# Forming the weight sums of the seven products by accumulating DMAs

## The chip, the cores and the metric

The kernel runs on one core of one Trainium2 chip. The metric is the device time of one execution in microseconds (us). TensorE (PE in the profile) multiplies, PEld is its weight load, VectorE is DVE, ScalarE is ACT, GpSimd is POOL, and SyncE (SP) issues most DMAs. An engine works through its own instructions in order; semaphores tie the engines and the DMAs together.

## The reference

One inference step of a one-layer streaming encoder with 1024 prompt tokens and 64 sample tokens (T = 1088 columns in all), D_MODEL = 1024, D_FF = 2816, everything in float32:

```python
def merge_branches(ret_o, ret_g, swa_o, gate_a, gate_b, w_ret_out, w_swa_out, w_mix_out):
    a = (rms_norm(ret_o) * silu(ret_g)) @ w_ret_out
    b = swa_o @ w_swa_out
    return (sigmoid(gate_a) * a + sigmoid(gate_b) * b) @ w_mix_out

rq, rk, rv, rg, sq, sk, sv, ga, gb = split(rms_norm(x, g_attn) @ w_in)
x = x + merge_branches(retention(rope(rq), rope(rk), rv), rg, window_attention(sq, sk, sv), ga, gb, ...)
x = x + cross_attn(rms_norm(x, g_cross), memory)
hn = rms_norm(x, g_ffn)
x = x + (silu(hn @ w_gate) * (hn @ w_up)) @ w_down
y = rms_norm(x, g_final)
```

The change touches the products with w_in, w_gate, w_up and w_down.

## The kernel before

Activations lie transposed: features on the 128 partitions, the 1088 tokens along the row. A float32 factor is split into two parts of the type float32r, hi and lo (`split`, L122): ScalarE casts hi (L123), VectorE subtracts it from the source to get lo (L124). A product is then three matmuls, hi·hi, hi·lo and lo·hi (L212, L213, L215).

The large products go in pairs of output tiles. A pair is a 2 x 2 block product: A is the weights' two output tiles (rows i) by two halves of the inner dimension (columns j), each block 128 partitions x 512 columns, 256 KB; B is the activations, two inner halves by two token halves of 544 columns. Instead of eight block products the kernel makes seven (Strassen's scheme in Winograd's form). One such group of seven is called a set here. There are 59 of them: 28 in the projection phase (q, k and v of the retention, queries and keys and values of the window attention, three gates), 21 for gate and up, 10 for the down projection. A set's seven products are named P1, P2, P6, P5, P7, P3, P4 in the order in which TensorE makes them. P1, P2 and P4 take the blocks A11, A12, A22 as they are; the others take sums of blocks. The sums of the activations (B11, B21, T2, T1, T3, B22, T4) are formed once for many sets.

For each set two raw tiles come from memory by SP (`load_raws`, L867; the down projection has its own loads): the first holds A11 and A12, the second A21 and A22. The pool has two such tiles (tag "raw", bufs=2), so one set's raws at a time. `weight_ops` (L173) splits the blocks that are used as they are, and POOL forms the sums in place: L190 A11 = A11 − A21, L191 A21 = A21 + A22, L193 A11 = A22 − A11, L196 A12 = A12 − A11. Each operand gets a tile "wq" (`new_op`, L144): five of them, and a sixth from the gates on; a tile is free when the product that read it is done, so splits run at most that many products ahead of TensorE. P7's operand is formed before P6's and P5's, though its product comes after them; `new_op` counts for this in its argument `ahead`.

`strassen` (L254) makes the products. Their results are joined on VectorE as they come out of PSUM: u1 is a copy of P1 (L262, ScalarE, once a set), u2 = P6 + u1, u5 = P5 + u2, u3 = P7 + u2 (L259), and each of the four output blocks is one more addition, in the callback `emit`, which each phase has of its own: in the projections `taken` (L591, its addition is L596), in gate and up `gate` and `up` (L1459, L1467), in the down projection `add` (L1542).

POOL also scales projections by the token's root mean square (L602), multiplies the gates a second time by it (L1465), forms the four sums of the hidden activations that go to memory for the down projection (L1480 to L1489) and adds to the outputs of the down projection (L1547). It issues a few DMAs, among them four stores of a gate (L697). The last group of the down projection has inner halves of three blocks (384 columns) and skips P2 and P4, so a set there has five products.

The order on each engine is made when the program is built: a scheduler that replays a timeline of its own places the instructions by their priority and expected time.

Of the kernel before, what the change touches and what calls it, by code (L numbers as in the profile page):

```python
# [109 lines left out]
class Kernel:  # L110
# [61 lines left out]

    def weight_ops(self, raws, n=512, skip=()):  # L173

        nc = self.nc
        half = [[raws[i][:, j * n:(j + 1) * n] for j in range(2)] for i in range(2)]
        (a11, a12), (a21, a22) = half
        add, sub = ALU.add, ALU.subtract
        w = {}

        def put(name, src):
# [3 lines left out]
            self.split(src, q[:, 0, :n], q[:, 1, :n])  # L185

        tt = nc.gpsimd.tensor_tensor
        put("P1", a11)
        put("P2", a12)
        tt(out=a11, in0=a11, in1=a21, op=sub)  # L190
        tt(out=a21, in0=a21, in1=a22, op=add)  # L191
        put("P7", a11)
        tt(out=a11, in0=a22, in1=a11, op=sub)  # L193
        put("P6", a11)
        put("P5", a21)
        tt(out=a12, in0=a12, in1=a11, op=sub)  # L196
        put("P3", a12)
        put("P4", a22)
        return w
# [54 lines left out]
    def strassen(self, w, x, emit, part=False):  # L254


        nc = self.nc
        u1, u2, u3, u5 = (self.fp.tile([P, 2, HC], F32, tag=t, bufs=1, name=t) for t in ("u1", "u2", "u3", "u5"))
        add = lambda out, a, b: nc.vector.tensor_tensor(out=out, in0=a, in1=b, op=ALU.add)  # L259
        ps = self.product(w, x, "P1", "B11")  # L260
        self.run_later()
        nc.scalar.copy(u1, ps)  # L262
# [307 lines left out]
    def project_phase(self):  # L570
        nc, tc, io = self.nc, self.tc, self.io
        with ExitStack() as ctx:
# [17 lines left out]

            def taken(ps, sb):  # L591
                o = staged()
                if sb is None:
                    nc.scalar.copy(o, ps)
                else:
                    nc.vector.tensor_tensor(out=o, in0=ps, in1=sb, op=ALU.add)  # L596
                return flat(o)

            def project(w, put, act=None, other=None):
                def emit(i, t, ps, sb):  # L600
                    o = taken(ps, sb)
                    (nc.vector if act is not None else nc.gpsimd).tensor_tensor(  # L602
# [12 lines left out]
            def rotated(w, h, j):  # L615

                done = {}

                def emit(i, t, ps, sb):
                    done[i, t] = taken(ps, sb)  # L620
                    if (1 - i, t) not in done:
# [16 lines left out]
            def values(w, h, by=self.strassen):  # L638
                def emit(i, t, ps, sb):
                    self.store(self.d_qkv[2, 2 * h + i, :, half(t)], taken(ps, sb))  # L640
                by(w, self.ops, emit)
# [233 lines left out]
    def load_ops(self, srcs):  # L875
        return self.weight_ops(self.load_raws(srcs))

# [555 lines left out]
    def gate_up(self, pairs):  # L1433
# [16 lines left out]
        for n, fs in enumerate(pairs):  # L1450
# [7 lines left out]

            def gate(i, t, ps, sb):  # L1459
                g = gates[i, t]  # L1460
                if sb is not None:
                    nc.vector.tensor_tensor(out=g, in0=ps, in1=sb, op=ALU.add)
# [4 lines left out]
            def up(i, t, ps, sb, h=h, save=save, n=n):  # L1467
                o = stage[4 + 2 * i + t]
                nc.vector.tensor_tensor(out=o, in0=ps, in1=sb, op=ALU.add)
                nc.vector.tensor_tensor(out=o, in0=o, in1=gates[i, t], op=ALU.mult)  # L1470
# [64 lines left out]
    def down(self, starts):  # L1535
# [28 lines left out]
        for gi, g in enumerate(GROUPS):  # L1564
            last = gi == len(GROUPS) - 1
            f0, n = starts[gi], g * P // 2
            for m in range(0, KT, 2):
                def emit(i, t, ps, sb, m=m):
                    add(m, i, t, ps, sb, nc.vector if last else nc.gpsimd)
                    if last and t == 1:  # L1570
# [15 lines left out]
                else:  # L1586
                    w = self.weight_ops(raws, n, ("P2", "P4") if last else ())
                    if m == KT - 2 and not last:
# [200 lines left out]
```

## Time and profile before

| | before |
|---|---|
| runs (us) | 2219.13, 2220.92, 2227.09 |
| median (us) | 2220.92 |
| span of the profiled execution (us) | 2221.3 |
| bytes moved by DMA | 290.84 MB, mean 131 GB/s |

The profiled execution's time is known as its span; it lies 0.4 us over the median of the three runs. The page lists each engine's busy time, the span in 40 slices, the DMA queues, the chain of work that ended last and the costliest groups of instructions. By slices (busy tenths, 55.5 us each):

```profile
PE   9999899999999998999999999999999999999996
DVE  8996778777677668765455555768777777778498
POOL 1221534342144122220000000014556555424440
DMA  5533445343444566326443112422343332385233
```

The sets lie in slices 1 to 15 (projections and gates) and 27 to 39 (gate and up, then down). A line of a group reads: line, engine, operation, out<-in, count | busy us, mean ns of one | idle time of the engine before them, and what ended it.

### The profile page before, as it was taken

What the parts mean: (1) busy time and instruction counts of PE and PEld (TensorE: products, weight loads), DVE (VectorE), ACT (ScalarE), POOL (GpSimd) and SP (SyncE); (2) the same over time, 40 slices, a digit from 0 to 9 for tenths busy, and PEclk for the clock granted to TensorE, in tenths of its full rate; (3) what the DMA queues carried; (4) which work ended last, traced back from release to release, by engine and by line L of the source; (5) the groups of instructions that cost most, each with busy time, mean ns of one, the idle gap of its engine ahead of it and who ended that gap; (6) DMA issues with size and microseconds to landing.
All of it is one profiled execution on the core that took longest, in us unless ns stands there. A gap on an engine that the chain in (4) does not pass through costs nothing. (4 is left out here: it accounts for less than half of the span.)

```text
span 2221.3 us, 41708 instructions
## 1 busy us (share of the span) xinstructions
PE 2165.5 (97%) x16435; PEld 2102.8 (95%) x16435; DVE 1573.4 (71%) x2654; ACT 887.8 (40%) x1900; POOL 643.1 (29%) x442
## 2 busy tenths in 40 slices
PE   9999899999999998999999999999999999999996
PEld 9999899999999996779999999999999999999996
DVE  8996778777677668765455555768777777778498
ACT  7334343435444446554133333333323222334243
POOL 1221534342144122220000000014556555424440
PEclk9999999999999999999999999999999999999998
DMA  5533445343444566326443112422343332385233
GB/s 202 161 112 113 119 130 143 108 135 112 151 158 164 171 216 216 99 69 210 137 151 101 69 40 66 140 89 89 120 134 102 103 119 94 129 289 170 87 113 110
DMA packets 181445, 290.84 MB, mean 131 GB/s; under 512 B 40290, under 2 KB 109314, under 8 KB 181250
## 3 DMA queue, kind: packets, MB, share of 16 engines
q1 hardware_dynamic: 176706, 278.74, 39.7%
q10 hardware_dynamic: 4032, 7.80, 0.9%
q8 instruction: 130, 2.13, 0.4%
q0 software_dynamic: 512, 1.64, 0.2%
q14 instruction: 65, 0.53, 0.1%
HBM read 196.95 MB, written 91.16 MB: 130 GB/s over the span
## 5 line engine op out<-in xcount | busy, mean ns | idle before, releaser
L123 ACT CAST wq<-raw 128x512 fp32r<-128x512 f32 (+1 forms) x499 | 303.6, 613 | 583.2 <-PE pq L215 251.0
L124 DVE TENSOR_TENSOR wq<-raw,wq 128x512 fp32r<-128x512 f32 (+1 forms) x499 | 436.7, 878 | 137.8 <-ACT wq L123 136.2
L212 PE MATMUL pq<-T,wq 128*128 128x272 f32 x1832 | 494.0, 289 | 3.9 <-ACT wq L123 1.9
L213 PE MATMUL pq<-T,wq 128*128 128x272 f32 x1832 | 494.1, 289 | 0.0
L213 PE MATMUL pq<-B,wq 128*128 128x272 f32 x1592 | 430.9, 290 | 6.9 <-DVE B L124 6.9
L212 PE MATMUL pq<-B,wq 128*128 128x272 f32 x1592 | 428.4, 289 | 1.9 <-DVE stage L596 1.9
L215 PE MATMUL pq<-T,wq 128*128 128x272 f32 x1832 | 384.7, 290 | 0.0
L190 POOL TENSOR_TENSOR raw<-raw 128x512 f32<-128x512 f32 (+1 forms) x59 | 80.8, 1370 | 956.1 <-DVE rs_r L301 481.9
L212 PEld LDWEIGHTS pq<-T,wq 128*128 128x128 f32 x1832 | 346.8, 189 | 5.7 <-issue 2.5
L213 PEld LDWEIGHTS pq<-T,wq 128*128 128x128 f32 x1832 | 346.4, 189 | 0.1
L215 PE MATMUL pq<-B,wq 128*128 128x272 f32 x1592 | 334.3, 290 | 0.0
L213 PEld LDWEIGHTS pq<-B,wq 128*128 128x128 f32 x1592 | 301.6, 190 | 9.0 <-DVE B L124 8.6
L212 PEld LDWEIGHTS pq<-B,wq 128*128 128x128 f32 x1592 | 301.2, 190 | 2.8 <-ACT wq L123 2.2
L215 PEld LDWEIGHTS pq<-T,wq 128*128 128x128 f32 x1832 | 291.8, 191 | 0.9 <-issue 0.7
L215 PEld LDWEIGHTS pq<-B,wq 128*128 128x128 f32 x1592 | 254.3, 191 | 0.0
L259 DVE TENSOR_TENSOR u<-pq,u 128x544 f32<-128x544 f32 x177 | 127.3, 719 | 108.4 <-PE pq L215 107.9
L193 POOL TENSOR_TENSOR raw<-raw 128x512 f32<-128x512 f32 (+1 forms) x59 | 83.2, 1411 | 130.7 <-DVE wq L124 122.2
L596 DVE TENSOR_TENSOR stage<-pq,u 128x544 f32<-128x544 f32 x112 | 80.2, 716 | 25.3 <-PE pq L215 20.7
L191 POOL TENSOR_TENSOR raw<-raw 128x512 f32<-128x512 f32 (+1 forms) x59 | 88.1, 1492 | 3.5
L990 POOL TENSOR_TENSOR t<-t,den 128x768 f32<-128x768 f32 (+2 forms) x34 | 48.9, 1439 | 131.5 <-DVE den L988 32.2
L196 POOL TENSOR_TENSOR raw<-raw 128x512 f32<-128x512 f32 (+1 forms) x59 | 81.3, 1379 | 4.4
L984 ACT ACTIVATE t<-t,nm 128x192 f32<-128x192 f32 (+2 forms) x136 | 58.9, 434 | 41.5 <-DVE nm L979 41.3
(388 smaller groups left out, 4614.6 us busy)
## 6 DMA issues: line engine op xcount, KB each, us to landing
hl<-d_op SPq DMA_DIRECT2D x85, 272.0 KB, 4.3
d_qkv<-stage SPq DMA_DIRECT2D x44, 272.0 KB, 2.4
d_op<-stage SPq DMA_DIRECT2D x44, 272.0 KB, 2.1
d_op<-ht SPq DMA_DIRECT2D x44, 272.0 KB, 3.4
raw<-w_gate SPq DMA_DIRECT2D x22, 512.0 KB, 3.5
raw<-w_up SPq DMA_DIRECT2D x22, 512.0 KB, 3.7
raw<-w_down SPq DMA_DIRECT2D x16, 512.0 KB, 4.1
d_gate<-stage ACTq DMA_DIRECT2D x28, 272.0 KB, 2.4
```

The costliest lines, as they stand in the source:

```text
L123: self.last_cast = self.nc.scalar.copy(hi, src).ins
L124: return self.nc.vector.tensor_tensor(out=lo, in0=src, in1=hi.bitcast(F32), op=ALU.subtract).ins
L190: tt(out=a11, in0=a11, in1=a21, op=sub)
L191: tt(out=a21, in0=a21, in1=a22, op=add)
L193: tt(out=a11, in0=a22, in1=a11, op=sub)
L196: tt(out=a12, in0=a12, in1=a11, op=sub)
L212: mm(ps[:, c, :HC], w[:, 0, ks], x[:, 0, cs], start=start, stop=False)
L213: mm(ps[:, c, :HC], w[:, 0, ks], x[:, 1, cs], start=False, stop=False)
L215: self.last_mm = mm(ps[:, c, :HC], w[:, 1, ks], x[:, 0, c * HC:(c + 1) * HC], start=False, stop=stop).ins
L259: add = lambda out, a, b: nc.vector.tensor_tensor(out=out, in0=a, in1=b, op=ALU.add)
L596: nc.vector.tensor_tensor(out=o, in0=ps, in1=sb, op=ALU.add)
L984: nc.scalar.activation(t[:, v, i, :nk], t[:, v, i, :nk], AF.Exp, bias=nm[:, v, i:i + 1], accum_out=den[:, v, i:i + 1])
```

## The change

POOL's four additions go. In their place stand four DMAs that POOL issues and that add their source onto their destination (`accum_op`), since such a DMA can only add, the sums are formed without minus signs, and the signs move to where the products are joined. Sums are built on A21's place: A21 + A22 (P5), then A11 + A21 + A22 on A11's place (P6), then A12 + A11 + A21 + A22 on A12's place (P3). For P7 A21 is loaded from memory again, by SP, and A11 is added onto it from memory. `new_op` is called in the order of the products, without `ahead`.

```diff
-    def weight_ops(self, raws, n=512, skip=()):
+    def weight_ops(self, raws, src, n=512, skip=()):
...
-        add, sub = ALU.add, ALU.subtract
+        blocks = lambda x: x.rearrange("p (k m) -> p k m", m=P)
...
-            q = w[name] = self.new_op({"P7": 2, "P6": -1, "P5": -1}.get(name, 0))
+            q = w[name] = self.new_op()
...
-        tt = nc.gpsimd.tensor_tensor
+        add = lambda out, x: nc.gpsimd.dma_start(blocks(out), x, accum_op=ALU.add)
+        add(a21, src(1, 1))
         put("P1", a11)
+        add(a11, blocks(a21))
         put("P2", a12)
-        tt(out=a11, in0=a11, in1=a21, op=sub)
-        tt(out=a21, in0=a21, in1=a22, op=add)
-        put("P7", a11)
-        tt(out=a11, in0=a22, in1=a11, op=sub)
+        add(a12, blocks(a11))
         put("P6", a11)
         put("P5", a21)
-        tt(out=a12, in0=a12, in1=a11, op=sub)
+        self.load(blocks(a21), src(1, 0))
+        add(a21, src(0, 0))
+        put("P7", a21)
         put("P3", a12)
         put("P4", a22)
```

`src(i, j)` names block Aij in memory. In `strassen` the joins keep their number and their operands, and some become subtractions:

```diff
-        add(u2, self.product(w, x, "P6", "T2"), u1)
-        add(u5, self.product(w, x, "P5", "T1"), u2)
+        self.join(u2, self.product(w, x, "P6", "T2"), u1, -1, 1)
+        self.join(u5, self.product(w, x, "P5", "T1"), u2, 1, -1)
         ps = self.product(w, x, "P7", "T3")
-        add(u3, ps, u2)
-        emit(1, 1, ps, u5)
-        emit(0, 1, self.product(w, x, "P3", "B22"), u5)
-        emit(1, 0, None if part else self.product(w, x, "P4", "T4"), u3)
+        self.join(u3, ps, u2)
+        emit(1, 1, ps, u5, -1, 1)
+        emit(0, 1, self.product(w, x, "P3", "B22"), u5, 1, -1)
+        emit(1, 0, None if part else self.product(w, x, "P4", "T4"), u3, 1, -1)
+
+    def join(self, out, ps, sb, sp=1, ss=1):
+
+        a, b = (ps, sb) if sp > 0 else (sb, ps)
+        self.nc.vector.tensor_tensor(out=out, in0=a, in1=b, op=ALU.add if sp == ss else ALU.subtract)
```

The callbacks pass the signs on; in the down projection `add` takes them as the operation of its two additions:

```diff
-        def add(m, i, t, ps, sb, by=nc.gpsimd):
+        op = {1: ALU.add, -1: ALU.subtract}
+        def add(m, i, t, ps, sb, sp=1, ss=1, by=nc.gpsimd):
             v = half(m + i, t).rearrange("p (b c) -> p b c", b=2)
             if ps is not None:
-                nc.vector.tensor_tensor(out=v, in0=ps, in1=v, op=ALU.add)
+                nc.vector.tensor_tensor(out=v, in0=v, in1=ps, op=op[sp])
             if sb is not None:
-                by.tensor_tensor(out=v, in0=sb, in1=v, op=ALU.add)
+                by.tensor_tensor(out=v, in0=v, in1=sb, op=op[ss])
```

More of the change, by code (lines that the diff above doesn't have):

```diff
@@ L589, in staged, with taken @@
                 return stage[(count[0] - 1) % len(stage)]
-            def taken(ps, sb):
+            def taken(ps, sb, *signs):
                 o = staged()
@@ L595, in taken, with emit @@
                 else:
[L596 removed]
+                    self.join(o, ps, sb, *signs)
                 return flat(o)
             def project(w, put, act=None, other=None):
[L600 to L601 removed]
+                def emit(i, t, ps, sb, *signs):
+                    o = taken(ps, sb, *signs)
                     (nc.vector if act is not None else nc.gpsimd).tensor_tensor(
@@ L638, in values, with emit @@
             def values(w, h, by=self.strassen):
-                def emit(i, t, ps, sb):
-                    self.store(self.d_qkv[2, 2 * h + i, :, half(t)], taken(ps, sb))
+                def emit(i, t, ps, sb, *signs):
+                    self.store(self.d_qkv[2, 2 * h + i, :, half(t)], taken(ps, sb, *signs))
                 by(w, self.ops, emit)
@@ L1457, in save, with gate @@
                 self.store(self.d_op[OPS.index(name), n], src)
-            def gate(i, t, ps, sb):
+            def gate(i, t, ps, sb, *signs):
                 g = gates[i, t]
                 if sb is not None:
-                    nc.vector.tensor_tensor(out=g, in0=ps, in1=sb, op=ALU.add)
+                    self.join(g, ps, sb, *signs)
                 nc.vector.tensor_tensor(out=g, in0=ps if sb is None else g, in1=r[t], op=ALU.mult)
@@ L1567, in down, with emit @@
             for m in range(0, KT, 2):
-                def emit(i, t, ps, sb, m=m):
-                    add(m, i, t, ps, sb, nc.vector if last else nc.gpsimd)
+                def emit(i, t, ps, sb, *signs, m=m):
+                    add(m, i, t, ps, sb, *signs, by=nc.vector if last else nc.gpsimd)
                     if last and t == 1:
```

18 lines of the change are left out of this document (9 added, 9 removed).

## The prediction

> **What bounds the kernel now.** I read the page's first lines, then busy time by stretch, then what TensorE waited for, then the group behind one line that comes once in every seven-product set.
>
> ```profile
> span 2221.3 us, 41708 instructions
> PE 2165.5 (97%) x16435; PEld 2102.8 (95%) x16435; DVE 1573.4 (71%) x2654; ACT 887.8 (40%) x1900; POOL 643.1 (29%) x442
> ```
>
> TensorE is busy for 97% of the span. All that can be won is the 55.8 us in which it isn't. The stretches (columns: stretch, its length, then busy time and instructions of each engine, granted clock, DMA share, GB/s) say where those are:
>
> ```profile
> 25.00:810.00 785.00, 768.20 (x6080) 756.03 (x6080) 587.37 (x991) 335.94 (x656) 241.81 (x163) 0.99 0.45 140
> 1500.00:1930.00 430.00, 429.10 (x3449) 428.91 (x3449) 320.62 (x384) 130.44 (x219) 238.54 (x162) 1.00 0.33 108
> 1930.00:2180.00 250.00, 244.29 (x1912) 242.37 (x1911) 190.97 (x263) 101.79 (x178) 99.55 (x67) 0.98 0.49 162
> ```
>
> These three stretches hold the sets that the change touches: 28 in the projections and gates, 21 in gate and up, 10 in the down projection. In the second one TensorE has no gap at all and runs at full clock. What TensorE waited for, in all (who, for whom: us, times, longest):
>
> ```profile
> PE pq L213 <- DVE B L124: 6.9, 6, 2.8
> PE pq L212 <- ACT wq L123: 1.9, 2, 1.3
> ```
>
> Only the second is a wait for weight operands, 1.9 us. POOL's sums never hold TensorE up. So the change can win almost nothing; the question is whether it costs.
>
> How much time a set has, by the copy of its first product (L262), which comes once a set (stretch 25 to 810, 1500 to 1930, 2100 to 2180; min/median/max ns, first and last start):
>
> ```profile
> L262 ACT COPY u<-pq x28: 590/607/614, 47.8 to 799.8; 128x544 f32<-128x544 f32 x28
> L262 ACT COPY u<-pq x20: 603/607/612, 1518.2 to 1912.0; 128x544 f32<-128x544 f32 x20
> L262 ACT COPY u<-pq x5: 598/605/607, 2114.1 to 2172.1; 128x544 f32<-128x544 f32 x5
> ```
>
> A set takes 752.0/27 = 27.9 us in the first stretch (other products lie between), 393.8/19 = 20.7 us in gate and up, where sets stand back to back (2.96 us a product), and 58.0/4 = 14.5 us in the last down group, whose sets have five products of three blocks.
>
> **The change, part by part.** *Removed:* four POOL additions a set.
>
> ```profile
> L124 DVE TENSOR_TENSOR wq<-raw,wq 128x512 fp32r<-128x512 f32 (+1 forms) x499 | 436.7, 878 | 137.8 <-ACT wq L123 136.2
> L190 POOL TENSOR_TENSOR raw<-raw 128x512 f32<-128x512 f32 (+1 forms) x59 | 80.8, 1370 | 956.1 <-DVE rs_r L301 481.9
> L193 POOL TENSOR_TENSOR raw<-raw 128x512 f32<-128x512 f32 (+1 forms) x59 | 83.2, 1411 | 130.7 <-DVE wq L124 122.2
> L191 POOL TENSOR_TENSOR raw<-raw 128x512 f32<-128x512 f32 (+1 forms) x59 | 88.1, 1492 | 3.5
> L196 POOL TENSOR_TENSOR raw<-raw 128x512 f32<-128x512 f32 (+1 forms) x59 | 81.3, 1379 | 4.4
> ```
>
> 80.8+83.2+88.1+81.3 = 333 us of POOL work goes, about 5.7 us a set, and VectorE's splits (878 ns in the mean, 0.68 us where POOL rests, below) get shorter. None of it is on TensorE's path, by the waits above: worth 0, at most the 1.9 us. The signs cost nothing either: each product's sum stays one VectorE instruction on the same operands, subtract for add.
>
> *Added:* four POOL-issued DMAs a set that add a 256 KB block onto another, and one SP load that fetches A21 a second time. The A12 addition runs beside the rest. The others form a chain: A21 += A22 from memory; A11 += A21; when that has read A21 and the P5 operand is split, A21 is loaded again; A21 += A11 from memory; split P7. Only then is the second raw buffer free, and since there are just two raw buffers, one pair, the next set's load waits for it. Before, the buffer was free as soon as the last operand was split, and no transfer stood between. So this is a loop: its length is the least time a set can take, however far ahead the splits run. The rows for its links (start us, us, engine, line):
>
> ```profile
> 1562.71 0.33 SPq L117 DMA_DIRECT2D raw<-w_gate  x1
> 1566.38 1.30 POOL L190 TENSOR_TENSOR raw<-raw 128x512 f32<-128x512 f32 x1 [4.25 <-DMA raw<-w_gate]
> 1581.01 0.59 SPq L117 DMA_DIRECT2D raw<-w_up  x1
> 1586.20 1.29 POOL L190 TENSOR_TENSOR raw<-raw 128x512 f32<-128x512 f32 x1 [4.00 <-DMA raw<-w_up]
> 1571.02 1.14 ACT L123 CAST wq<-raw 128x512 fp32r<-128x512 f32 x2 [2.68 <-POOL raw L193]
> 1565.39 0.68 DVE L124 TENSOR_TENSOR wq<-raw,wq 128x512 fp32r<-128x512 f32 x1
> 1577.46 0.61 ACT L262 COPY u<-pq 128x544 f32<-128x544 f32 x1
> ```
>
> - Load of the second raw to its first user: 1566.38−1562.71 = 3.7 us and 1586.20−1581.01 = 5.2 us, mean 4.4.
> - In the changed program's order ScalarE casts P6 before P5 in most sets, so the reload waits from the landing of A11 for two casts (1.14), a split (0.68) and hand-overs (0.3, estimate): 2.2.
> - The reload, 256 KB on SP, by its nearest rows, 2.8 to 3.2, taken 2.9.
> - After the last addition: a cast and a split of P7 with a hand-over, 1.5; the splits of P3 and P4, which mostly stand behind P7 in that order, 2 x 0.68 = 1.4.
>
> Three additions remain. No accumulating DMA is in this trace. The rows for what POOL issues, the same store on ScalarE's queue, and SP's 256 KB and 384 KB loads (KB each, median us to landing; the fourth row is min/median/max of the first):
>
> ```profile
> d_gate<-stage POOLq DMA_DIRECT2D x4, 272.0 KB, 3.4
> d_mv<-swin POOLq DMA_DIRECT2D x2, 128.0 KB, 4.9
> o_mv<-swin POOLq DMA_DIRECT2D x2, 128.0 KB, 5.8
> DMA to landing us min/median/max: 2.8/3.4/4.2
> d_gate<-stage ACTq DMA_DIRECT2D x28, 272.0 KB, 2.4
> vf<-d_qkv SPq DMA_DIRECT2D x16, 256.0 KB, 3.2
> ks<-d_qkv SPq DMA_DIRECT2D x16, 256.0 KB, 2.8
> qs<-d_qkv SPq DMA_DIRECT2D x16, 256.0 KB, 2.9
> raw<-w_down SPq DMA_DIRECT2D x8, 384.0 KB, 3.2
> ```
>
> POOL's issue costs 1.0 us more than ScalarE's for the same store (3.4 against 2.4). By the nearest size an addition takes 3.4; a read from memory is some 0.5 slower than the store (2.9 against 2.4), and the destination must be read as well. Bounds: 2.8, the quickest POOL row, and 5.8, the slowest median. I take 4.2 each, nearer to the row of its size: 12.6 for three.
>
> The loop: 4.4 + 12.6 + 2.2 + 2.9 + 1.5 + 1.4 = 25.0 us.
>
> By the fit in the Trainium skill, DMA: Bandwidth & Descriptors, "Anatomy of one DMA — SWDGE (gpsimd) path" (about 2.0 us fixed plus bytes at 436 GB/s), a 256 KB transfer would take an estimated 2.6 us and the loop 12.4 + 7.8 = 20.2, under the 20.7 that a set has. The trace's 272 KB row, 3.4 against the fit's 2.6, speaks against it, and the fit is of plain transfers.
>
> *Where it lands.* Gate and up: 25.0 − 20.7 = 4.3 us a set. The lead that the six operand buffers give doesn't pay for it: the load at 1562.71 is for the set whose first product ends at 1577.46, so its fifth, P7, starts 3 x 2.96 us later, at 1586.3, 23.6 us after the load; load, chain and P7's split (25.0 − 1.4) take just that. So 21 x 4.3 = 90 us.
>
> Down: in two groups of three full sets, four intervals at 4.3, 17 us. The last group's sets split P5 before P6 and have no P4: 3.2 + 12.6 + 2.7 + 1.5 + 0.7 = 20.7 against 14.5, 6.2 in each of four intervals, 25, of which I take 15, since six buffers hold more than a whole such set.
>
> Projections and gates: 25.0 is under 27.9, hidden by retention and the memory products between the sets. What remains is order: the reload stands in SP's queue until P5 is split, and retention's loads (ks, qs, vf) and the stores of q and k stand behind it; on POOL, additions waiting for each other hold up the scaling by rstd and the gate's second multiplication. Bounds 0 and about 40 us (16 sets with retention beside them, 2.5 us for each); I take 8, since those loads, too, are issued well ahead.
>
> Sum: 90 + 17 + 15 + 8 = 130; 2221.3 + 130 = 2351, and as the profiled execution lies 0.4 us over the median of the runs, 2350 us.
>
> **The rivals.**
> *The loop fits.* With all three additions at 2.8 us the loop is 12.4 + 8.4 = 20.8, as long as a set: 0.1 x 21 = 2 in gate and up, some 5 in the last group: 2221 to 2231 us, not slower by more than a measurement can tell. It decides at 2.95 us an addition: 12.4 + 8.85 = 21.25, 0.5 us over a set, 11 us in 21. For it: the additions end in SBUF, while the POOL rows end in memory. Against it: at 272 KB half of POOL's landings took over 3.4. By the page's fit above this would be the outcome.
> *Dearer additions.* At 5.8 each the loop is 12.4 + 17.4 = 29.8. Gate and up lose 9.1 x 21 = 191, down some 55, and now also the first stretch, 1.9 x 27 = 51: 2518 us. For it: reading the destination too, more DMA load (five blocks more a set on queues that are a third to a half busy), POOL rows at 4.9 and 5.8 for half the size. Against it: those came in pairs, one behind the other.
> *Faster.* POOL and VectorE relieved, TensorE's small waits gone: 2 to 10 of the 55.8 us, about 2212. Against it: no wait of TensorE leads to POOL, and where POOL is busiest TensorE has no gap.
>
> **How the numbers follow.** A change of 0.5% (11 us) is about the least a measurement of this kernel tells. Forecast 0.65, fits 0.14, dearer 0.16, faster 0.05. Fits lies within 0.5% but for 0.01: faster 0.05, same 0.13, slower 0.82. The likeliest's own range, additions from 3.3 to 5.2 us (loops of 22.3 and 28.0), is 2270 to 2440. The range of 2222 to 2525 takes in the upper part of the first rival and most of the dearer case, leaving out some 0.19.
>
> **What would show it.** Right: gaps of TensorE before the fifth product of a set in gate and up, ended by the cast of P7 (L123), POOL raw issues landing in about 4.2 us, L262 copies about 25 us apart there and still 28 in the first stretch. Wrong: landings under 3 us and copies 20.7 apart (fits), 29 apart and the first stretch stretched too (dearer), or gaps that are ended by something other than weight operands, such as retention's loads or POOL's scaling.

## The result, and the profile after

| | before | after |
|---|---|---|
| median of the runs (us) | 2222.5 | 2527.4 |
| span of the profiled execution (us) | 2221.3 | 2525.5 |

The changed kernel is slower by a ratio of 1.137 (95% interval 1.136 to 1.139). The forecast was 2350 us with a range up to 2525: the direction was right, the size less than half of the 304 us by which the two profiled spans differ.

The head of the page of the kernel after:

```profile
span 2525.5 us, 42314 instructions
PE 2266.5 (90%) x16435; PEld 2185.9 (87%) x16435; DVE 1485.8 (59%) x2654; ACT 871.7 (35%) x1898; POOL 492.8 (20%) x442
```

Two things are to be seen. TensorE now stands idle for 2525.5 − 2266.5 = 259 us, against 55.8: 203 us more. And it is busy for 2266.5 − 2165.5 = 101 us more with the same 16435 matmuls. The windows of the kernel after (columns as in the prediction) show what goes with it: in all three stretches with sets the granted clock has dropped, most where TensorE's idle share is largest (52 of 260 us in the third).

```profile
25.00:910.00 885.00, 796.48 (x6006) 776.36 (x6007) 536.38 (x979) 322.82 (x648) 171.54 (x162) 0.95 0.61 161
1640.00:2180.00 540.00, 463.89 (x3388) 456.20 (x3386) 273.98 (x367) 116.36 (x205) 181.97 (x160) 0.93 0.54 138
2220.00:2480.00 260.00, 207.65 (x1495) 203.50 (x1494) 143.03 (x199) 74.34 (x132) 70.12 (x61) 0.91 0.55 142
```

Where the time went is read from the copies of the first product, one a set (min/median/max ns, first and last start), first of after:

```profile
L262 ACT COPY u<-pq x28: 590/607/620, 43.6 to 910.5; 128x544 f32<-128x544 f32 x28
L262 ACT COPY u<-pq x21: 601/603/607, 1638.8 to 2179.4; 128x544 f32<-128x544 f32 x21
L262 ACT COPY u<-pq x10: 598/605/614, 2218.8 to 2465.5; 128x544 f32<-128x544 f32 x10
```

and two rows of before that go beyond those of the prediction (all 21 copies in gate and up, and the ten of down):

```profile
L262 ACT COPY u<-pq x21: 601/607/612, 1518.2 to 1935.3; 128x544 f32<-128x544 f32 x21
L262 ACT COPY u<-pq x10: 598/607/610, 1979.0 to 2172.1; 128x544 f32<-128x544 f32 x10
```

| stretch | before (us) | after (us) | more | forecast |
|---|---|---|---|---|
| up to the first copy | 47.8 | 43.6 | −4 | 0 |
| projections and gates, first to last copy | 752.0 | 866.9 | 115 | 8 |
| attention between, to the next copy | 718.4 | 728.3 | 10 | 0 |
| gate and up, first to last copy | 417.1 | 540.6 | 124 | 90 |
| down, from there to its last copy | 236.8 | 286.1 | 49 | 32 |
| from there to the end | 49.2 | 60.0 | 11 | 0 |

A set takes 540.6/20 = 27.0 us in gate and up (before 20.9, forecast 25.0) and 866.9/27 = 32.1 in the projections and gates (before 27.9, forecast unchanged).

One set in gate and up, from the timeline of the kernel after (start, us, engine, line, in brackets the idle time of the engine before it):

```profile
1748.82 2.10 SPq L117 DMA_DIRECT2D raw<-w_gate  x2
...
1755.57 0.88 POOL L187 DMA_DIRECT2D raw<-w_gate  x1 [5.55 <-DVE u L278]
1755.57 0.72 DVE L278 TENSOR_TENSOR u<-pq,u 128x544 f32<-128x544 f32 x1
1760.31 0.87 POOL L187 DMA_DIRECT2D raw<-raw  x1 [3.86 <-DMA raw<-w_gate]
...
1763.64 1.14 ACT L123 CAST wq<-raw 128x512 fp32r<-128x512 f32 x2 [10.07 <-DMA raw<-raw]
1764.29 0.69 DVE L124 TENSOR_TENSOR wq<-raw,wq 128x512 fp32r<-128x512 f32 x1 [8.01 <-ACT wq L123]
...
1765.54 0.71 DVE L278 TENSOR_TENSOR stage<-u,pq 128x544 f32<-128x544 f32 x1
...
1766.88 0.33 SPq L117 DMA_DIRECT2D raw<-w_gate  x1
1770.07 0.87 POOL L187 DMA_DIRECT2D raw<-w_gate  x1 [4.99 <-DVE stage L278]
1774.36 1.66 ACT L123 CAST wq<-raw 128x512 fp32r<-128x512 f32 x3 [9.58 <-DMA raw<-w_gate]
1777.50 0.94 SPq L117 DMA_DIRECT2D raw<-w_up  x2
```

This is read twice. First as the loop: load at 1748.82; A21's addition at 1755.57, A11's at 1760.31, P6's cast at 1763.64, the reload at 1766.88, the last addition at 1770.07, P7's cast at 1774.36, and the next set's load at 1777.50. Each transfer starts soon after the one before has landed, and from load to load it is 28.7 us (27.0 in the mean). Second as two queues: ScalarE stands 10.07 us in front of P6's cast; VectorE, done with u5 of the set being multiplied (1755.57), stands 8.01 us in front of P6's split. That split is for the set to come. Queued behind it are u3 and the sum of P7 (the row at 1765.54) of the set being multiplied, and TensorE needs their accumulators back. So an operand that isn't wanted yet stops the sums that are.

The windows around that place (same columns) show TensorE's share of it: a gap (2.56 us busy of 4.60, and it goes on into the next row), then 6.6 us at half the granted clock, then 1.00 again:

```profile
1759.30:1763.90 4.60, 2.56 (x21) 2.34 (x19) 0.00 (x0) 0.26 (x1) 0.87 (x1) 1.00 0.39 77
1764.10:1770.70 6.60, 4.31 (x19) 4.34 (x20) 5.91 (x9) 0.68 (x2) 1.49 (x3) 0.50 0.58 164
1771.00:1777.00 6.00, 6.00 (x50) 6.00 (x50) 1.99 (x2) 2.17 (x4) 5.84 (x4) 1.00 0.78 232
```

Matmuls a microsecond of busy time: 19/4.31 = 4.4 at half clock, 50/6.00 = 8.3 after. So this gap is paid for twice.

What TensorE waited for in gate and up after (1640 to 2180 us; us, times, longest):

```profile
PE pq L213 <- DVE stage L278: 42.6, 16, 4.6
PE pq L213 <- ACT u L262: 13.6, 10, 2.9
PE pq L213 <- ACT stage L1469: 7.9, 3, 3.5
PE pq L213 <- ACT wq L123: 4.2, 1, 4.2
```

Of these waits only the last, 4.2 us, is for a weight operand. The others are for accumulators that VectorE and ScalarE hadn't emptied. The third row names the gate's Silu (L1469), which reads no accumulator, but in each of its three cases a sum of VectorE (L278) had ended 0.15 us before TensorE went on, so it belongs to these. And POOL's issues for the set there (KB each, median us to landing):

```profile
raw<-raw POOLq DMA_DIRECT2D x40, 256.0 KB, 3.3
raw<-w_gate POOLq DMA_DIRECT2D x20, 256.0 KB, 4.0
```

An addition from SBUF takes 3.3 us, one from memory 4.0, both below the 4.2 assumed.

### The profile page after: what moved, and what is told of

The parts are those of the page before. It is cut to its first block, busy times and chain, and to the rows that moved or that the text cites. A ratio compares the mean times of both kernels' runs of the same rounds, so it can differ in the third digit from the quotient of the medians.

```text
span 2525.5 us, 42314 instructions
## 1 busy us (share of the span) xinstructions
PE 2266.5 (90%) x16435; PEld 2185.9 (87%) x16435; DVE 1485.8 (59%) x2654; ACT 871.7 (35%) x1898; POOL 492.8 (20%) x442
## 5 line engine op out<-in xcount | busy, mean ns | idle before, releaser
L124 DVE TENSOR_TENSOR wq<-raw,wq 128x512 fp32r<-128x512 f32 (+1 forms) x499 | 371.2, 758 | 613.2 <-ACT wq L123 608.9
L213 PE MATMUL pq<-T,wq 128*128 128x272 f32 x1832 | 527.6, 305 | 150.6 <-ACT wq L123 83.7
L123 ACT CAST wq<-raw 128x512 fp32r<-128x512 f32 (+1 forms) x499 | 292.5, 613 | 940.2 <-DMA raw<-raw 383.9
L214 PE MATMUL pq<-T,wq 128*128 128x272 f32 x1832 | 520.0, 301 | 0.0
L213 PEld LDWEIGHTS pq<-T,wq 128*128 128x128 f32 x1832 | 370.3, 202 | 164.9 <-ACT wq L123 89.4
L213 PE MATMUL pq<-B,wq 128*128 128x272 f32 x1592 | 441.4, 296 | 27.3 <-DVE stage L278 22.6
L214 PE MATMUL pq<-B,wq 128*128 128x272 f32 x1592 | 440.8, 295 | 6.8 <-DVE B L124 6.8
L216 PE MATMUL pq<-T,wq 128*128 128x272 f32 x1832 | 404.2, 302 | 0.0
L214 PEld LDWEIGHTS pq<-T,wq 128*128 128x128 f32 x1832 | 369.8, 202 | 0.4 <-issue 0.3
L216 PE MATMUL pq<-B,wq 128*128 128x272 f32 x1592 | 339.3, 294 | 0.0
L213 PEld LDWEIGHTS pq<-B,wq 128*128 128x128 f32 x1592 | 310.6, 195 | 30.8 <-issue 20.8
L214 PEld LDWEIGHTS pq<-B,wq 128*128 128x128 f32 x1592 | 310.7, 195 | 8.1 <-DVE B L124 8.0
L216 PEld LDWEIGHTS pq<-T,wq 128*128 128x128 f32 x1832 | 309.5, 202 | 1.8 <-DVE wq L124 1.3
L216 PEld LDWEIGHTS pq<-B,wq 128*128 128x128 f32 x1592 | 260.3, 196 | 0.0
L187 POOL DMA_DIRECT2D raw<-raw x118 | 103.0, 873 | 434.9 <-DMA raw<-raw 190.3
L187 POOL DMA_DIRECT2D raw<-w_up x22 | 19.5, 886 | 505.4 <-DVE hx L1337 479.7
L278 DVE TENSOR_TENSOR stage<-pq,u 128x544 f32<-128x544 f32 x147 | 105.4, 717 | 17.5 <-PE pq L216 8.8
L278 DVE TENSOR_TENSOR u<-pq,u 128x544 f32<-128x544 f32 x118 | 83.4, 717 | 46.4 <-PE pq L216 46.1
L156 PE MATMUL pd<-xc,wq 128*128 128x256 f32 (+1 forms) x256 | 74.4, 291 | 0.0
L158 PE MATMUL pd<-xc,wq 128*128 128x256 f32 (+1 forms) x256 | 74.1, 289 | 0.0
L157 PE MATMUL pd<-xc,wq 128*128 128x256 f32 (+1 forms) x256 | 73.7, 288 | 0.0
```

Of the source, the lines that this page charges most:

```text
L123: self.last_cast = self.nc.scalar.copy(hi, src).ins
L124: return self.nc.vector.tensor_tensor(out=lo, in0=src, in1=hi.bitcast(F32), op=ALU.subtract).ins
L156: mm(ps, wh, xh, start=start, stop=False)
L157: mm(ps, wh, xl, start=False, stop=False)
L158: self.last_mm = mm(ps, wl, xh, start=False, stop=stop).ins
L187: add = lambda out, x: nc.gpsimd.dma_start(blocks(out), x, accum_op=ALU.add)
```

## The experiments

In each diff below, lines of the changed kernel are taken out or added, unless another kernel is named. The table at the end of this section has all times side by side.

### A buffer of its own for P7's sum, in gate and up

```diff
-        self.load(blocks(a21), src(1, 0))
-        add(a21, src(0, 0))
-        put("P7", a21)
+        a7 = a21 if self.own is None else self.own.tile([P, 512], F32, tag="own", bufs=2, name="own")[:, :n]
+        self.load(blocks(a7), src(1, 0))
+        add(a7, src(0, 0))
+        put("P7", a7)
```

> In gate and up (from the second pair of blocks on) A21 is loaded again into a buffer of its own, so that P7's sum no longer holds the raw pair; the DMAs and their bytes stay the same. Theory of the loop (the chain of transfers through the one pair of raw buffers sets the time of a set): the loop loses its reload, last addition and P7's split, 27.0 - 10 = 17 us, under the 20.7 of a set; the copies of the first product in gate and up go back from 27.0 to 20.7 us apart, and the whole from 2527 to about 2400 us (20 intervals x 6.3 = 126), projections and down unchanged. Theory of traffic (more DMA work and more issues on POOL slow everything): nothing changes, 2527 +- 10. Theory of the order in the queues (the reload waits at the head of SP's queue): the reload's wait for P5 is gone too, so this run would also come back; it doesn't tell the two apart.

2499 us; sets of 25.9 us. A miss: taking the reload and the last addition out of the raw pair's loop won 28 us, not 126. So the chain through P7 is not the only thing that binds. (The projections, which this edit leaves as they are, took 855.2 us from first to last copy in place of 866.9; over four kernels with the same code there it is 855.2 to 868.9, so a difference of some 14 us in that stretch shows little.)

### P7's sum by POOL, no reload

```diff
-        self.load(blocks(a21), src(1, 0))
-        add(a21, src(0, 0))
+        nc.gpsimd.tensor_tensor(out=a21, in0=a11, in1=a22, op=ALU.subtract)
         put("P7", a21)
```

> The reload and the last addition are left out; P7's sum is formed by one POOL subtraction in SBUF (A11 after its addition, less A22), three accumulating DMAs a set remain. Theory of the loop: 27.0 less reload (2.9), addition (4.1) and two hand-overs (1.4) plus one POOL operation (1.4) is about 20, at or under the 20.7 of a set in gate and up, and about 24 under the 27.9 in the projections: 2225 to 2260 us. Theory of traffic: two of the five added transfers gone, so about two fifths of the 305 us, 2405 us. Clock: if the half-speed pieces only follow TensorE's gaps, the mean granted clock goes back from 0.951 to about 0.985 with the gaps; if they come from the additions themselves it stays near 0.95 to 0.97.

2388 us, ratio 1.075 (1.073 to 1.077), mean granted clock 0.967. Neither theory's number in gate and up: sets of 25.4 us, though the loop through the raw pair should be about 20. The projections and gates gave back 63 of their 115 us (804.1 us from first to last copy).

### All four sums by POOL, with the new signs and the new order

```diff
-        add = lambda out, x: nc.gpsimd.dma_start(blocks(out), x, accum_op=ALU.add)
-        add(a21, src(1, 1))
+        tt = nc.gpsimd.tensor_tensor
+        tt(out=a21, in0=a21, in1=a22, op=ALU.add)
...
-        add(a11, blocks(a21))
+        tt(out=a11, in0=a11, in1=a21, op=ALU.add)
...
-        add(a12, blocks(a11))
+        tt(out=a12, in0=a12, in1=a11, op=ALU.add)
...
-        self.load(blocks(a21), src(1, 0))
-        add(a21, src(0, 0))
+        tt(out=a21, in0=a11, in1=a22, op=ALU.subtract)
```

> The new signs and the new order of the operands, but all four sums by POOL in SBUF as before, with no added DMA. All theories: the signs and the place of P7 cost nothing, 2222 +- 10 us. If the new order alone costs (P7's sum now last, three operands after P7 in place of six), up to 2260.

2220.1 us, ratio 0.9998 (0.9986 to 1.0009). The signs and the new place of P7 cost nothing; the whole loss comes with the DMAs.

### Additions that nothing waits for

To the kernel before, four accumulating DMAs a set were added, first of weight blocks from memory onto a scratch in memory:

```diff
+    def idle(self, src, n):
+        t = self.dram.tile([P, 4, 512], F32, tag=f"idle{self.idles % 4}", name="idle")
+        self.idles += 1
+        b = lambda x: x.rearrange("p (k m) -> p k m", m=P)
+        for k, (i, j) in enumerate(((1, 1), (0, 1), (0, 0), (1, 0))):
+            self.nc.gpsimd.dma_start(b(t[:, k, :n]), src(i, j), accum_op=ALU.add)
```

> The kernel before, with four POOL-issued accumulating DMAs of a 256 KB (192 KB in the last down group) weight block for each set, onto a scratch in memory that nothing reads. Theory of the loop: nothing waits for them, so 2222 to 2240 us. Theory of traffic: about the same DMA work and the same four issues on POOL as in the changed kernel, so most of the 305 us, 2400 to 2527 us.

2600 us, and no test of either theory: as nothing ties these DMAs to their set, the order made at build time put them at the front: POOL's DMA queue moves 60.83 MB in the first 560 us and 1.64 MB in all the rest. Two things can still be read. While they run, the DMA engines are busy for 95% of the time and the first five intervals between sets are 75 to 119 us long; in gate and up, where none is left, the sets are 20.9 apart.

So a second form ties them to the set: four additions of A22, from SBUF onto the scratch.

```diff
+        for k in range(4):
+            self.nc.gpsimd.dma_start(t[:, k, :n], a, accum_op=ALU.add)
...
+        self.aside(a22, n)
         put("P3", a12)
```

> The kernel before, with four more POOL-issued accumulating DMAs a set, of A22 from SBUF onto a scratch in memory that nothing reads, queued after POOL's last sum of the set: the issues and the transfers without anything that waits for their landing but the buffer's reuse. Theory of waits (chains, order): 2222 to 2260 us, gaps of TensorE under 80 us. Theory of traffic and of POOL's issue time: 2400 to 2527 us.

2367 us: 145 us lost, though no operand waits for a landing (only the next load into A22's buffer does). That lies between the two forecasts, nearer to that of traffic and of POOL's issue time (2400 to 2527). The timeline of POOL in that kernel shows how the issues act:

```profile
1815.42 2.69 POOL L177 DMA_DIRECT2D aside<-raw  x3 [4.50 <-DMA raw<-w_gate]
1819.47 0.87 POOL L177 DMA_DIRECT2D aside<-raw  x1 [1.37 <-issue]
1820.03 1.62 POOL L196 TENSOR_TENSOR raw<-raw 128x512 f32<-128x512 f32 x1
```

The issues stand in POOL's queue ahead of the set's sums, and four of them in a row hold POOL from 1815.42 to about 1820: the sums start 4.6 us late. Sets alternate between about 18 and 30 us there, 24.4 in the mean, and what TensorE waits for most in gate and up (1565 to 2055 us) are weight operands, with 12.3 us more for the casts (L123) behind this row:

```profile
PE pq L222 <- DVE wq L124: 25.2, 11, 2.9
```

So POOL's issue time has a price of its own when it stands at the head of the chain to the operands. How much of the 145 us the traffic took was not separated.

### The order of the splits

The splits from P6 on are queued, on ScalarE and VectorE, behind the last sum of the set before (`newest` finds the last instruction of each of the two engines):

```diff
-        put("P6", a11)
...
+        with ExitStack() as behind:
+            for ins in self.marks_set:
+                behind.enter_context(self.tc.issue_after(ins))
+            put("P6", a11)
...
         emit(1, 0, None if part else self.product(w, x, "P4", "T4"), u3, 1, -1)
+        self.marks_set = self.newest()
```

> The changed kernel, with only the issue order altered: the splits of a set's P6, P5, P7, P3 and P4 are queued on ScalarE and VectorE behind the last sum of the set before, in place of between its sums. Theory of the order (a split that waits for an addition's landing stands in front of the sums that free the accumulators TensorE needs next): its waits on the stage and u sums in gate and up go, but P7's chain now starts later, so sets come down from 27.0 to about 25 us there, what the loop through the raw pair allows: 2440 to 2500 us in all. Theory of the loop alone: the splits come later, so the raw pair is free later: sets longer than 27.0, 2527 to 2600 us.

2590 us, 63 more; sets of 28.3 us. That is the range of the theory of the loop, by which the later splits make the raw pair free later.

> Both: a buffer of its own for P7's sum in gate and up, and the splits from P6 on behind the last sum of the set before. Theory of the order and the loop together (each hides the other): sets of gate and up from 25.9 back to 20.7 to 21.5 us, about 100 us off the 2499 of the first alone, 2380 to 2420 us. Theory of traffic: no change from 2499. If only the order counts, the same as the run with the order alone.

2493 us, 6 less than with the buffer alone, which is no clear gain for one execution of each, but sets of gate and up at 24.0 in place of 25.9; the projections lost most of what was won there. The expected 20.7 didn't come. The timeline of that kernel shows, in one set, what follows what once P7 is out of the way:

```profile
1834.27 0.82 SPq L117 DMA_DIRECT2D raw<-w_up  x2
...
1842.50 0.91 POOL L188 DMA_DIRECT2D raw<-w_up  x1 [3.83 <-DVE wq L124]
1847.23 0.88 POOL L188 DMA_DIRECT2D raw<-raw  x1 [3.83 <-DVE stage L289]
1851.19 0.86 POOL L188 DMA_DIRECT2D raw<-raw  x1 [3.08 <-DMA raw<-raw]
...
1857.80 0.33 SPq L117 DMA_DIRECT2D raw<-w_gate  x1
```

Load, A21's, A11's and then A12's addition follow each other at 1834.27, 1842.50, 1847.23 and 1851.19; behind the splits of P3 and P4 the next load goes at 1857.80: 23.5 us. A12's addition doesn't run beside the rest, it is a second arm of the same loop.

> P7's sum by POOL (no reload, three additions by DMA a set), and the splits from P6 on behind the last sum of the set before. Theory of the order and the loop: load, two additions and hand-overs take about 13 us and the splits follow within 5, under 20.7: gate and up back to 20.7, the projections to about 28, 2230 to 2290 us. Theory of traffic: no change from 2388.

2375 us, ratio 1.069 (1.068 to 1.071), 12 us less than without the order. Sets of 24.7 us, where 20.7 was expected; what holds them there was not settled.

### Two pairs of raw buffers, in gate and up

All DMAs stay. Two of the six buffers that hold operands for the down projection make room.

```diff
+    def new_raw(self):
+        self.raws += 1
+        if self.raw2 is not None and self.raws // 2 % 2:
+            return self.raw2.tile([P, 1024], F32, tag="raw2", bufs=2, name="raw2")
+        return self.wp.tile([P, 1024], F32, tag="raw", bufs=2, name="raw")
```

> The changed kernel with two pairs of raw buffers in gate and up from the second pair of blocks on (room from two of the six buffers that hold operands for the down projection); every DMA, every issue and every byte stays. Theory of the loop through the raw pair (load, A21, A11 and either P7's chain or A12 and P3, all before the next load): the loads run a set ahead, sets of gate and up go from 27.0 to 20.7 to 21.5 us, the granted clock there from 0.93 back to about 1.0, and the whole to 2400 to 2420 us. Theory of traffic and of POOL's issue time: 2527 +- 10. Theory of the order alone (splits in front of sums): with the data a set ahead no split waits, so it agrees with the loop.

2435 us, ratio 1.096 (1.094 to 1.099): 92 us back, all of it in gate and up, where the 21 copies now take 446.8 us (22.3 a set, with the first two still on one pair). The window of this kernel from 1720 us on, then the same DMAs' landings and TensorE's waits in it:

```profile
1720.00:2090.00 370.00, 361.70 (x2874) 359.60 (x2874) 221.80 (x310) 99.65 (x176) 159.69 (x136) 1.00 0.62 163
```

```profile
raw<-raw POOLq DMA_DIRECT2D x34, 256.0 KB, 4.3
raw<-w_up POOLq DMA_DIRECT2D x17, 256.0 KB, 4.0
```

```profile
PE pq L219 <- DVE stage L284: 4.5, 3, 2.2
PE pq L219 <- ACT u L268: 3.8, 7, 1.0
```

The additions land no sooner (4.3 from SBUF, 4.0 from memory) and move more bytes a second (163 GB/s against 138), yet TensorE idles for 8.3 of 370 us and the clock is back at 1.00. Traffic, POOL's issue time and the latency of an addition are all there and cost little once a set doesn't have to wait for the set before (some 21.7 us a set from the third interval on, against 20.9 before). In gate and up that shows the single pair of raw buffers as the cause; both readings above, the loop and the splits in front of sums, rest on it.

### The projections and gates

> The change in the projections and gates alone, gate, up and down as before. If the losses of the stretches add up: 2222 + 110 (first product of the last gate set at 910 against 800 us) + 10 (in the attention after it) = 2342 us, mean granted clock about 0.975. If a part of the loss in gate and up is handed on from the projections: under 2330 us.

The change in the projections and gates alone (gate, up and down as before): 2337 us, +115. The stretches' losses add up; this part is real and not handed on.

```diff
-        self.load(blocks(a21), src(1, 0))
+        nc.gpsimd.dma_start(blocks(a21), src(1, 0))
```

> A21 is loaded again by POOL's queue in place of SP's, so that nothing of retention, queries, keys and gates stands behind it on SP. If the loss in the projections and gates (set spacing 32.6 and 30.5 against 28.1 and 27.4) comes from SP's queue: 40 to 100 us less there, 2430 to 2490 us. If it comes from the chain's own length: POOL's queue is held for the reload instead and the time stays or grows, 2520 to 2570 us.

2523 us; 852.6 us from first to last copy against 866.9. That is 14 of the 115 us, no more than this stretch differs between kernels with the same code in it. So SP's queue, which the forecast had feared here beside POOL's, is not where most of the loss comes from; what the reload costs on POOL's queue instead is contained in the figure.

### One addition at a time

The base is the kernel with all four sums by POOL (2220 us); one of them is put back as a DMA.

```diff
-        tt(out=a21, in0=a21, in1=a22, op=ALU.add)
+        add(a21, src(1, 1))
```

> Of the four sums only the first, A21 += A22, is an accumulating DMA; A11's, A12's and P7's are formed by POOL in SBUF. It stands at the head of the chain to P6 and adds 4.0 + 0.7 - 1.3 = 3.4 us to it. Theory of the loop through the raw pair alone: load 4.4 + 4.7 + POOL's sums 4 + splits 4 is about 17, under 20.7: 2222 to 2235 us. Theory of the chain's start and the issue order (P6's split stands in front of sums of the set before, so a later P6 stops VectorE though the pair would be free in time): some of the 305 us already with this one, 2240 to 2300 us. Theory of traffic: a fifth of it, 2283.

2305 us, ratio 1.038 (1.037 to 1.040).

```diff
-        tt(out=a12, in0=a12, in1=a11, op=ALU.add)
+        add(a12, blocks(a11))
```

> Only A12's sum is an accumulating DMA, the same issue and 256 KB as in the run with A21's alone, but at the chain's end: only P3's operand waits for it. Theories of the loop and of the order: 2222 to 2235 us, clearly less than the run with A21's alone if the place in the chain decides. Theory of traffic and of POOL's issue time: the same as with A21's alone.

2212.7 us, ratio 0.9963 (0.9950 to 0.9975): faster than both kernels.

```diff
-        tt(out=a21, in0=a11, in1=a22, op=ALU.subtract)
+        self.load(blocks(a21), src(1, 0))
+        add(a21, src(0, 0))
```

> Only P7's operand comes by DMA (the second load of A21 and one accumulating DMA); the three other sums are POOL's. P6 and P5 are as early as before, the raw pair is held longer: load 4.4 + POOL's sums 2.8 + casts 2.2 + reload 2.9 + 0.7 + addition 4.1 + P7's split 1.5 + P3, P4 1.4 = 20.0. Theory of the loop: just under the 20.7 of a set in gate and up, 2222 to 2270 us. Together with the runs of one addition it shows whether the losses add up (sum far below 305) or whether only the whole chain exceeds the set. Theory of traffic: two fifths, 2344.

2328 us, ratio 1.048 (1.046 to 1.050): sets of 23.1 us, dearer than its loop of 20.0 us allowed, and nearest to the 2344 of the theory of traffic. A11's sum alone as a DMA was not run.

An accumulating DMA of 256 KB costs 85 us at the head of the chain, and one at its end wins 8. They differ in their source too: A21's addition reads memory and landed after 3.9 to 4.0 us, A12's reads SBUF and landed after 3.4. But 0.6 us is little beside the difference, and the order of the splits below changes the price of A21's with the DMA as it is. So the number of transfers isn't what decides; their place, with the order behind it, is. One thing that A12's DMA changes is seen in VectorE's splits in gate and up (1500 us on; min/median/max ns), first in the kernel before, then with A12's DMA:

```profile
L124 DVE TENSOR_TENSOR wq<-raw,wq x144: 674/1012/1864, 1507.5 to 1934.4; 128x512 fp32r<-128x512 f32 x144
```

```profile
L124 DVE TENSOR_TENSOR wq<-raw,wq x143: 679/693/1882, 1502.3 to 1925.2; 128x512 fp32r<-128x512 f32 x143
```

The median falls from 1012 to 693 ns (from 1215 in the base). Where the 8 us come from is not shown: gate and up is no faster than before (sets of 21.0 us), and the projections and gates take 743.9 us against 747.0 in the base.

A21's DMA alone leaves a loop of about 17 us by the estimate above, and still costs 3 us a set. Two more kernels alter only the order of the splits in it, behind the last sum of the set before, or one product earlier:

```diff
         emit(0, 1, self.product(w, x, "P3", "B22"), u5, 1, -1)
+        self.marks_set = self.newest()
```

> The run with A21's addition alone as a DMA (2305 us), with the splits of P6, P5, P7, P3 and P4 queued on ScalarE and VectorE behind the last sum of the set before. Theory of the order (a later P6 costs because its split stands in front of sums of the set before, while the raw pair itself would be free in time): sets of gate and up from 23.9 back to about 21, 2225 to 2260 us in all. Theory that the operand's chain itself is too long, whatever the order: no gain, 2290 to 2330 us.

> The same with the splits queued one product earlier, behind the sum of P3 of the set before. Theory of the order: also 2225 to 2270 us, nearer the lower end if the later place lets P6 come too late for TensorE. Theory of the chain's length: 2290 to 2330 us.

2278 us (ratio 1.025, 1.022 to 1.027) and 2249 us (1.012, 1.010 to 1.014). The second takes back 56 of the 85 us, with sets of gate and up at 21.4 after 23.9; TensorE's waits there, without the order (1515 to 2005 us) and with it (1515 to 1950 us):

```profile
PE pq L213 <- ACT stage L1469: 19.6, 9, 3.9
PE pq L213 <- DVE stage L278: 14.2, 13, 2.2
```

```profile
PE pq L220 <- DVE wq L124: 1.6, 3, 0.6
```

The waits for accumulators, 33.8 us, are gone. (L1469 is again the Silu; in all nine cases a sum, L278, had ended 0.15 us before TensorE went on.) A later P6 did most of its harm in gate and up through the fixed order, by standing in front of sums that were due. Behind the last sum the splits come too late instead: there TensorE waits 13.9 us for L123.

### All runs

The third column is the time from the first to the last of the 28 copies in the projections and gates, the fourth the mean spacing in gate and up. A kernel for which no ratio is given above was executed once.

| kernel | us | projections, gates | set in gate and up |
|---|---|---|---|
| before | 2222.5 | 752.0 | 20.9 |
| after | 2527.4 | 866.9 | 27.0 |
| own buffer for P7 | 2499.5 | 855.2 | 25.9 |
| own buffer, splits behind | 2493.5 | 886.2 | 24.0 |
| splits behind alone | 2590.2 | 886.8 | 28.3 |
| two raw pairs in gate and up | 2435.4 | 868.9 | 22.3 |
| reload by POOL's queue | 2522.6 | 852.6 | 27.2 |
| change in projections and gates only | 2337.0 | 859.5 | 20.9 |
| P7 by POOL | 2387.7 | 804.1 | 25.4 |
| P7 by POOL, splits behind | 2375.4 | 792.1 | 24.7 |
| all sums by POOL | 2220.1 | 747.0 | 21.1 |
| only P7 by DMA | 2328.4 | 779.6 | 23.1 |
| only A21 by DMA | 2305.3 | 766.5 | 23.9 |
| only A21, splits behind the last sum | 2277.6 | 758.3 | 22.5 |
| only A21, splits behind P3's sum | 2249.1 | 757.3 | 21.4 |
| only A12 by DMA | 2212.7 | 743.9 | 21.0 |
| before, additions aside from SBUF | 2366.7 | 800.4 | 24.4 |
| before, additions in memory | 2600.2 | 1084.5 | 20.9 |

## Why the prediction was right or wrong

*What bounds the kernel, and the signs: right.* All sums by POOL in the new form take the time of before, so the signs and the new order were worth nothing. The removed work was put at 0, at most 1.9 us; the run with A12's sum alone as a DMA won 8, so that term may be too small, by little beside 304 us.

*The price of an addition: right, a little high.* 4.2 us was taken, 3.3 and 4.0 were measured. The rival in which the loop fits, which the Trainium skill's fit (DMA: Bandwidth & Descriptors, "Anatomy of one DMA — SWDGE (gpsimd) path") would have brought about with an estimated 2.6 us, fell on these rows. (That section doesn't say which transfers its fit is of; that they are plain ones is the forecast's assumption.) The rival of dearer additions, whose 2518 us lie near the result, fell too: no addition in gate and up came near 5.8 us in the median. Its time was right by accident.

*The loop in gate and up: the mechanism right, its size too small.* Forecast 25.0 us, measured 27.0; two pairs of buffers removed nearly all of it with all DMAs in place. The steps, from the rows of the raw tiles in gate and up, in the mean of 19 intervals between loads of the second raw:

| step | forecast (us) | measured (us) |
|---|---|---|
| load to A21's addition | 4.4 | 5.4 |
| to A11's addition | 4.2 | 4.7 |
| to P6's cast | 4.2 | 3.4 |
| to the reload | 2.2 | 2.2 |
| to the last addition | 2.9 | 3.5 |
| to P7's cast | 4.2 | 4.4 |
| to the next load | 2.9 | 3.2 |
| sum | 25.0 | 26.8 |

The load was mis-sized most: SP's loads of w_up land after 5.1 us in the median there, 3.7 before. The hand-overs to POOL were left out: some 0.7 us pass between a landing and POOL's next issue, behind the load, A21's addition and the reload. A11's addition, 0.8 us cheaper than forecast, hides a part of that. The loop also has a second arm, through A12's addition, which "runs beside the rest" in the forecast; with P7's arm taken out and the splits moved it took 23.5 us in the set shown.

*"Projections and gates: 25.0 is under 27.9, hidden": wrong, and the largest error*, 8 us against 115. Here the mean time of a set was taken for slack. It isn't, for two reasons. The intervals between the copies were not all 27.9 us before, but 19.0 to 38.0; six of the 27 lay under the 25.0 of the forecast's own loop. These six lost 43 us, and the other 21 lost 72, so the short intervals are the smaller part. And TensorE was busy for 98% of that stretch before (768.20 of 785 us), with products whose operands and sums go through the same ScalarE and VectorE. When a cast waits for an addition, all that is queued behind it waits. TensorE's waits, 40 to 905 us, first after, then the largest of before:

```profile
PE pq L213 <- ACT wq L123: 32.9, 12, 5.5
PE po L156 <- ACT ss L123: 16.8, 5, 7.6
PE pb L867 <- ACT ret_o L863: 13.9, 8, 4.5
```

```profile
PE pb L862 <- ACT ret_o L858: 7.9, 4, 2.9
```

The first is the weight operands themselves, 32.9 us where the kernel before shows no such wait in that window. The second and third are retention's own operands, late by 30.7 us together against 8.3 before (0.4 for ss). The queues that the forecast looked at were SP's and POOL's; taking the reload off SP's gave back 14 us. The losses there by the single runs are 14.5 us with A21's addition alone (766.5 − 752.0), 27.6 with P7's alone, 52 with the three that don't serve P7, 115 with all. A21's falls to 5.3 with the splits behind P3's sum; both of these are no more than kernels with the same code in that stretch differ by. How the 115 divide between order, loop and added traffic in the full kernel stays open: a second pair of buffers was not tried in that stretch, and the additions aside, for which no operand waits, cost 48 us there too (800.4 − 752.0).

*The step that failed in kind* is thus the assumption, behind "hidden", that an operand which comes late only matters when TensorE wants it. The sign the forecast named, gaps ended by P7's cast, was seen in gate and up for only 4.2 us; the gaps were ended by sums (42.6 us for L278) that stood behind a split. Gaps ended by something other than weight operands are what the forecast had named as a sign of being wrong.

*The clock: not in the forecast at all.* 101 of the 304 us are the same matmuls taking longer, at a mean granted clock of 0.951 in place of 0.989. With the gaps gone (two raw pairs, 1.00 in the window) it came back, with the DMAs still running.

*Down and the end:* 49 us against 32, and 11 against 0. No run takes these apart, so why they cost more stays open, as do the 10 us in the attention between.

## What to carry to other kernels

Price a change of latency by its place: an accumulating DMA of 256 KB lost 85 us at the head of a chain and 29 there with the splits in another order (2249.1 − 2220.1); one at the chain's end won 8. Before calling a delay hidden, look at what stands behind the waiting instruction in its engine's fixed order, since a wait for data of the next round can stop the sums of this one; and count the loop through the buffers with every hand-over and every arm. Where TensorE is nearly full, reckon with a slower clock behind the gaps as well as with the gaps.

## What the runs showed of the hardware

A gap shorter than the stretch of slow clock that follows it can be enough to start that stretch. The windows of the kernel after in a gap of 2.3 us, 1819.1 to 1821.4, and behind it:

```profile
1819.10:1821.40 2.30, 0.00 (x0) 0.02 (x1) 2.20 (x5) 0.09 (x1) 0.40 (x1) 1.00 0.68 110
1822.10:1825.40 3.30, 3.30 (x17) 3.30 (x16) 1.96 (x3) 0.62 (x1) 1.45 (x2) 0.50 0.57 217
1825.50:1829.00 3.50, 3.50 (x30) 3.49 (x28) 0.21 (x1) 0.87 (x2) 3.42 (x4) 1.00 1.09 182
```

Soon after TensorE is busy again the clock is halved, for 17 matmuls in 3.30 us, then it is whole, with 30 in 3.50. The Trainium skill (TensorE: Matmul & The Clock Gate, "Part 1: The HAM clock gate (the "warmup" mystery)") puts the drop after an idle window of about 3.4 us; here a gap of 2.3 us was enough. Not every such gap is: of the 23 gaps of 1.9 to 2.9 us in the trace of the kernel after, 17 were followed by half clock within 4.5 us.

Four accumulating DMAs issued in a row by POOL took 2.69 us for three, then 1.37 us of standing still, then 0.87 for the fourth: about 4.9 us of POOL in all, nearly as much as the four sums in SBUF that such DMAs replace in the change (5.7 us a set).
